# Moving two families of DMA issues off SyncE: in-projection spills to ScalarE, late modulation weights to GpSimd

## The chip, the cores and the metric

The kernel runs on one core of one Trainium2 chip. The metric is device time in microseconds (us); the shown figure is the median of three runs. Five instruction streams run beside each other and each is in order: PE (TensorE), DVE (VectorE), ACT (ScalarE), POOL (GpSimd) and SP (SyncE). A DMA is issued by one of the last three; the issue stands in that engine's stream like any other instruction and waits there for its semaphores.

## The reference

One block of a hybrid model, 512 tokens by 1024 channels, all in float32:

```
cond = silu(c)
mod = cond @ w_ada + b_ada                       # 6 x 1024: shift, scale, gate, twice
h = rms_norm(x, norm1) * (1 + scale1) + shift1
p = h @ w_in                                     # q,k,v | z | beta,a | RWKV columns | gate_a | gate_b
y_a = gated_deltanet(qkv, z, ...) @ w_branch_gdn # chunks of 64 tokens, 8 heads
y_b = rwkv7_time_mix(p_b, ...) @ w_branch_rwkv
x = x + gate1 * ((sigmoid(gl_a) * y_a + sigmoid(gl_b) * y_b) @ w_out)
h = rms_norm(x, norm2) * (1 + scale2) + shift2
x = x + gate2 * conv_glu(h, w_ffn_in, conv, w_ffn_out)
return rms_norm(x, norm_f)
```

## The kernel before

Everything is held transposed, channels on the 128 partitions and the 512 tokens along the free axis. A product of a weight tile with the activations is made of 24 matmuls of 128x128 by 128x512 (8 tiles of the inner dimension, 3 matmuls each): weights and activations are split into a high and a low part in fp32r, `whi`/`wlo` and `hh`/`hl`, and `mm3` (lines 182 to 191) issues high x high (L186), high x low (L189) and low x high (L190). A weight tile comes by a 512 KB DMA into `raw` (two buffers, L156); ACT makes `whi` (L145) and DVE makes `wlo` (L148).

The products form a queue, and `stream` works it off a few matmuls at a time: the chunk recurrences call `fill(n)` between their own small matmuls. So the recurrences of GatedDeltaNet (lines 742 to 788, steps L754, L762, L775, L776) and of RWKV-7 (lines 862 to 899, steps L868, L874, L887, L888) run inside the stream of products. Each recurrence is preceded by a triangular solve (`solve`, lines 544 to 610): its 32x32 blocks go out to DRAM and back in another layout (`lsc`, L556 and L559), DVE works 30 elimination steps (L567, L569), and the result makes a second trip through DRAM (`tsc`, `usc`).

Two things of this program are touched by the change:

- **The spills.** Four groups of products are not used at once: z (`zsc`), the two merge gates (`asc`, `bsc`) and the GatedDeltaNet branch (`ysc`), 28 tiles in all. `spill` copies the PSUM bank to a buffer `tmp_sp` on ACT (L404) and stores that to DRAM (L405); the loads back are L840 (`zsc`) and L944 to L946.
- **The late modulation weights.** Of the 48 modulation columns groups, 16 are made in the prologue. The other 32 come in halves through one single buffer `wada`: 64 times `ada_half` loads 256 KB (L208), and DVE multiplies by `cond` and sums (L209, an instruction of 128x512 and a short one that reads the sum). With one buffer, a load can't be issued before the L209 ahead of it is done.

The author's code gives an order, but the framework's scheduler sets the place of each instruction in its engine's stream, by its own model of their cost. An instruction whose issuer changes can so move on every engine. Between L817 and L842, named below, lies this work: L812 multiplies for the RWKV chunk matrices, DVE masks them (L817, L816), POOL clears parts of them (L578, L821), and DVE and ACT normalize the GatedDeltaNet output (L833), gate it with z (L842) and split it (L148 into `tmp_acc` and `tmp_sq`); this is the input of the branch products. A2 (L998) is a small vector of modulation factors.

Of the kernel before, what the change touches and what calls it, by code (L numbers as in the profile page):

```python
# [55 lines left out]
def body(ctx, tc, io, out, tap=lambda name, ap: None):  # L56
    nc = tc.nc
    pe, act, dve, pool, sp = nc.tensor, nc.scalar, nc.vector, nc.gpsimd, nc.sync
# [42 lines left out]
    def tmp(tag, bufs=2):  # L101
        return tp.tile([128, 512], F32, name=f"tmp_{tag}", tag=tag, bufs=bufs)
# [14 lines left out]
    def col(name, j=0, w=1):  # L117
        o = COLS[name][0] + j
        return cols[:, o:o + w]
# [85 lines left out]
    def ada_half(j, u):  # L205
        w = wp.tile([128, T], F32, name="wada", tag="wada")
        part = slice(T * u, T * u + T)
        sp.dma_start(w, io["w_ada"][j][:, part])  # L208
        i = dve.tensor_tensor_reduce(out=w, in0=w, in1=cond[:, part], scale=1.0,  # L209
                                 scalar=half[:, j:j + 1] if u else col("b_ada", j), op0=ALU.mult, op1=ALU.add,  # L210
                                 accum_out=(mod if u else half)[:, j:j + 1])
        if last["gate"] is not None:
            tc.add_manual_dep(i.ins, last["gate"].ins.name, after, reason="place")
            last["gate"] = None
# [15 lines left out]
    def stream():  # L230
        while queue:
            it = queue.pop(0)
            for _ in range(min(it["late"], len(ada_rest))):
                ada_half(*ada_rest.pop(0))
            for i, q in enumerate(it["pieces"]):
                for a in (it["pieces"][i:] + [b for nx in queue[:2] for b in nx["pieces"]])[:2]:
                    if a["w"] is None:
                        a["w"] = weights(a["src"], a["n"] * 128, a["spare"])
                if it["halves"]:
                    continue  # L240
                if i == 0:
                    p = it["psum"]()
                for k in range(q["n"]):
                    at = q["k0"] + k
                    mm3(p, q["w"], k, it["xs"][at], at == 0, at == it["n"] - 1)
                    if at == it["n"] - 1:
                        it["evac"](p)
                        done.add(it["label"])
                    yield
            for u in range(2 if it["halves"] else 0):  # L250
                part = slice(H * u, H * u + H)
                p = it["psum"]()[:, 0:H]
                for q in it["pieces"]:
                    for k in range(q["n"]):
                        at = q["k0"] + k
                        mm3(p, q["w"], k, [x[:, part] for x in it["xs"][at]], at == 0, at == it["n"] - 1)
                        yield
                it["evac"](p, u, part)
                done.add(it["label"])
# [141 lines left out]
    def spill(dst):  # L401
        def f(p):
            o = tmp("sp")
            act.copy(o, p)  # L404
            sp.dma_start(dst, o)  # L405
        return f

    kqs = slot2(0)
# [123 lines left out]
    def hs(e):  # L532
        return slice(64 * e, 64 * e + 64)
# [210 lines left out]
    for c in range(NC):  # L744
# [12 lines left out]
        for ct, e, r in heads():  # L757
            o = hs(1 - e)
# [7 lines left out]
        if c < NC - 1:  # L766
            p = q4(pc()[:, 0:256])
            for ct, e, r in heads():
                o = hs(1 - e)
# [226 lines left out]
    while ada_rest:  # L996
        ada_half(*ada_rest.pop(0))
# [167 lines left out]
```

## Time and profile before

| | |
|---|---|
| time, median of 3 runs | 939.75 us (938.65 to 940.68) |
| the profiled execution, its own time | 938.37 us |
| its span on the core | 936.4 us |
| PE busy | 878.2 us, 94% |
| DVE / ACT / POOL busy | 532.2 / 424.3 / 107.3 us |
| granted TensorE clock, mean | 0.98 |
| DMA queue 1 (all issues of SP) | 125.88 MB, 42.4% of 16 engines |

PE carries the program. The span is read as PE's work plus the places where PE stands; the first 17 us (loads and the first norm) and the last 8 us have a mostly idle PE, and the rest of its idle time lies in short gaps of about one us in the recurrences, the solves and the merge.

### The profile page before, as it was taken

The numbers are of one execution on the slowest core, as the hardware profiler recorded it, in microseconds if no ns is written. First come the engines' busy times: TensorE is split into PE (matmuls) and PEld (weight loads), VectorE is DVE, ScalarE is ACT, GpSimd is POOL, SyncE is SP. The second block draws the span as 40 slices with busy tenths as digits, with TensorE's granted clock in tenths as the row PEclk, the third lists the DMA queues.
The fourth block names the chain that finished last, engine by engine and source line by source line (L and its number), as shares of the span: only waits on it lengthen the run. The fifth ranks groups of instructions, "written<-read, shape, count | busy, mean of one in ns | idle before, by whom it ended". The sixth has DMA issues, their size and how long they took to land.

```text
span 936.4 us, 13900 instructions
## 1 busy us (share of the span) xinstructions
PE 878.2 (94%) x5459; PEld 687.0 (73%) x5459; DVE 532.2 (57%) x850; ACT 424.3 (45%) x691; POOL 107.3 (11%) x99
## 2 busy tenths in 40 slices
PE   2999989999999988999998999999999999999996
PEld 1886577676666666777665788888888888888885
DVE  5987859724796777245378537465444445332233
ACT  5368443734654838622466435343333333232231
POOL 1000310000361300001233320000000000010112
PEclk9999999998999989899999999999999999999998
DMA  9841254454233366744537542322332332533322
GB/s 340 284 161 57 79 138 158 130 138 137 89 91 100 86 219 225 185 143 159 176 120 255 178 153 83 106 97 90 100 103 90 96 108 90 176 100 101 101 85 90
DMA packets 81695, 126.77 MB, mean 135 GB/s; under 512 B 26109, under 2 KB 42877, under 8 KB 81566
## 3 DMA queue, kind: packets, MB, share of 16 engines
q1 hardware_dynamic: 81630, 125.88, 42.4%
q8 instruction: 43, 0.70, 0.3%
q14 instruction: 22, 0.18, 0.1%
HBM read 110.66 MB, written 14.68 MB: 134 GB/s over the span
## 4 chain that ended last, share of the span: by engine, by line
PE 70%; DVE 10%; ACT 8%; issue 6%; DMA 3%; POOL 2%; SPq 0%; DVEq 0%; ACTq 0%; POOLq 0%
PE ps_mm L186 19%; PE ps_mm L189 18%; PE ps_mm L190 18%; PE ps_pc L181 3%; DVE wlo L148 2%; ACT slot L615 2%; ACT tmp_rs L94 1%; PE ps_pc L186 1%; PE ps_pc L189 1%; PE ps_pc L190 1%; PE ps_pa L186 1%; ACT whi L145 1%; PE ps_pa L189 1%; PE ps_pa L190 1%; PE ps_pa L600 1%
## 5 line engine op out<-in xcount | busy, mean ns | idle before, releaser
L186 PE MATMUL ps_mm<-hh,whi 128*128 128x512 f32 (+1 forms) x714 | 291.2, 409 | 7.6 <-ACT hh L304 3.4
L190 PE MATMUL ps_mm<-hh,wlo 128*128 128x512 f32 (+1 forms) x714 | 280.8, 395 | 2.2 <-DVE wlo L148 2.2
L189 PE MATMUL ps_mm<-hl,whi 128*128 128x512 f32 (+1 forms) x714 | 280.8, 394 | 0.0
L148 DVE TENSOR_TENSOR wlo<-raw,whi 128x1024 fp32r<-128x1024 f32 (+2 forms) x140 | 161.1, 1151 | 184.5 <-ACT whi L145 178.2
L145 ACT CAST whi<-raw 128x1024 fp32r<-128x1024 f32 (+2 forms) x140 | 137.1, 979 | 246.5 <-PE ps_mm L189 188.0
L186 PEld LDWEIGHTS ps_mm<-hh,whi 128*128 128x128 f32 x714 | 135.4, 190 | 47.0 <-issue 7.0
L190 PEld LDWEIGHTS ps_mm<-hh,wlo 128*128 128x128 f32 x714 | 135.5, 190 | 34.2 <-DVE wlo L148 4.0
L189 PEld LDWEIGHTS ps_mm<-hl,whi 128*128 128x128 f32 x714 | 135.8, 190 | 29.9 <-issue 4.8
L186 PE MATMUL ps_mm<-slot,whi 128*128 128x512 f32 (+1 forms) x154 | 59.1, 385 | 2.7 <-ACT hh L145 1.5
L190 PE MATMUL ps_mm<-slot,wlo 128*128 128x512 f32 (+1 forms) x154 | 59.5, 386 | 1.8 <-DVE wlo L148 1.8
L189 PE MATMUL ps_mm<-slot,whi 128*128 128x512 f32 (+1 forms) x122 | 45.5, 373 | 0.2 <-DVE slot L148 0.2
L209 DVE CUSTOM_DVE_ANT_0 wada<-wada,cond,cols 128x512 f32<-128x512 f32 x32 | 25.0, 782 | 33.5 <-DMA wada<-in_w_ada 33.5
L190 PEld LDWEIGHTS ps_mm<-slot,wlo 128*128 128x128 f32 x154 | 29.7, 193 | 9.3 <-DVE wlo L148 4.2
L186 PEld LDWEIGHTS ps_mm<-slot,whi 128*128 128x128 f32 x154 | 29.7, 193 | 9.3 <-ACT hh L145 1.9
L186 PE MATMUL ps_mm<-slotd,whi 128*128 128x512 f32 (+1 forms) x96 | 36.4, 380 | 0.0
L190 PE MATMUL ps_mm<-slotd,wlo 128*128 128x512 f32 (+1 forms) x96 | 36.1, 376 | 0.0
L189 PE MATMUL ps_mm<-slotd,whi 128*128 128x512 f32 (+1 forms) x96 | 36.1, 376 | 0.0
L1040 DVE TENSOR_TENSOR tmp_sg<-tmp_acc,ps_mm 128x512 f32<-128x512 f32 x20 | 13.8, 688 | 35.6 <-PE ps_mm L190 35.5
L394 DVE SCALAR_TENSOR_TENSOR tmp_acc<-ps_mm,cols,tmp_acc 128x511 f32<-128x511 f32 (+2 forms) x44 | 32.8, 746 | 0.7
L973 POOL COPY tmp_rs<-tmp_sq 128x512 f32<-128x512 f32 x2 | 2.1, 1068 | 267.4 <-ACT tmp_sq L970 267.4
L94 ACT ACTIVATE tmp_acc<-tmp_acc 128x512 f32<-128x512 f32 x22 | 13.9, 631 | 41.5 <-DVE tmp_acc L394 41.4
L975 POOL TENSOR_TENSOR tmp_rs<-tmp_rs,tmp_sq 128x512 f32<-128x512 f32 x12 | 19.5, 1623 | 103.8 <-ACT tmp_sq L970 103.8
(266 smaller groups left out, 1286.7 us busy)
## 6 DMA issues: line engine op xcount, KB each, us to landing
raw<-in_w_in SPq DMA_DIRECT2D x40, 512.0 KB, 4.0
raw<-in_w_fi SPq DMA_DIRECT2D x37, 512.0 KB, 3.5
wada<-in_w_ada SPq DMA_DIRECT2D x64, 256.0 KB, 2.9
raw<-in_w_fo SPq DMA_DIRECT2D x16, 512.0 KB, 3.5
slot<-in_w_ada SPq DMA_DIRECT2D x10, 512.0 KB, 8.5
slot<-in_xT SPq DMA_DIRECT2D x16, 256.0 KB, 4.2
raw<-in_w_out SPq DMA_DIRECT2D x8, 512.0 KB, 3.6
raw<-in_w_in SPq DMA_DIRECT2D x8, 448.0 KB, 4.5
```

The costliest lines, as they stand in the source:

```text
L94: i = act.activation(*a, **k)
L145: i = act.copy(hi, src)
L148: j = eng.tensor_tensor(lo, src, hi.bitcast(F32), op=ALU.subtract)
L181: last["step"] = pe.matmul(*a, **k)
L186: i = pe.matmul(p, hi, xh, start=start, stop=False)
L189: pe.matmul(p, hi, xl, start=False, stop=False)
L190: pe.matmul(p, lo, xh, start=False, stop=stop)
L209: i = dve.tensor_tensor_reduce(out=w, in0=w, in1=cond[:, part], scale=1.0, scalar=half[:, j:j + 1] if u else col("b_ada", j), op0=ALU.mult ...
L394: dve.scalar_tensor_tensor(acc[:, i:], p[:, :T - i], w[:, taps - 1 - i:taps - i], acc[:, i:], op0=ALU.mult, op1=ALU.add)
L615: (act.copy if e == c or quiet else dve.tensor_copy)(place(e, 2 * b + c), p[hs(c), :, e, :])
L975: pool.tensor_tensor(sums[0], sums[0], sq, op=ALU.add)
L1040: dve.tensor_tensor(t, accs[j], p, op=ALU.mult)
```

## The change

The issuing engine of two DMA calls is another one. Sizes, buffers and computations are the same.

```
     def ada_half(j, u):
         w = wp.tile([128, T], F32, name="wada", tag="wada")
         part = slice(T * u, T * u + T)
-        sp.dma_start(w, io["w_ada"][j][:, part])
+        pool.dma_start(w, io["w_ada"][j][:, part])
...
     def spill(dst):
         def f(p):
             o = tmp("sp")
             act.copy(o, p)
-            sp.dma_start(dst, o)
+            act.dma_start(dst, o)
         return f
```

All 64 loads of `wada` stand in POOL's stream now, and all 28 spills in ACT's. The first load of `wada` needs nothing and stands near the start of POOL's stream. The scheduler moves DVE's L209 to earlier places as well: 19 of them stood behind the first L874 of the RWKV recurrence, and now none does.

On DVE, at the end of the GatedDeltaNet recurrence, the normalization (L833) and gating (L842) stood like this before; the `tmp_acc` and `tmp_sq` rows are the split that the branch products read:

```order
L209 ISA wada,mod<-wada,cond,half 128x512
L209 ISA mod 128x1
L833 SCALAR_TENSOR_TENSOR slotd_459<-slotd_459,cols,tmp_rs 128x512
L148 TENSOR_TENSOR wlo<-raw,whi 128x1024
L833 SCALAR_TENSOR_TENSOR slotd_459<-slotd_459,cols,tmp_rs 128x512 x3
L842 TENSOR_TENSOR tmp_rs<-slotd_459,tmp_sg 128x512 x2
L148 TENSOR_TENSOR tmp_acc<-tmp_rs,slot_2750 128x512 x2
L148 TENSOR_TENSOR wlo<-raw,whi 128x512
L842 TENSOR_TENSOR tmp_rs<-slotd_459,tmp_sg 128x512 x2
L560 TENSOR_SCALAR slot_2673<-slot_2673 128x1024
L148 TENSOR_TENSOR tmp_sq<-tmp_rs,slot_2750 128x512 x2
```

The same rows on DVE now, as far as the first two L842:

```order
L209 ISA wada,mod<-wada,cond,half 128x512
L209 ISA mod 128x1
L833 SCALAR_TENSOR_TENSOR slotd_459<-slotd_459,cols,tmp_rs 128x512 x2
L148 TENSOR_TENSOR wlo<-raw,whi 128x1024
L209 ISA wada,half<-wada,cond,cols 128x512
L209 ISA half 128x1
L833 SCALAR_TENSOR_TENSOR slotd_459<-slotd_459,cols,tmp_rs 128x512
L148 TENSOR_TENSOR wlo<-raw,whi 128x512
L833 SCALAR_TENSOR_TENSOR slotd_459<-slotd_459,cols,tmp_rs 128x512
L209 ISA wada,mod<-wada,cond,half 128x512
L209 ISA mod 128x1
L842 TENSOR_TENSOR tmp_rs<-slotd_459,tmp_sg 128x512 x2
```

Two L209 that were not there stand between the normalizations and the gating, and two more follow before the `tmp_sq` split. From the last L754 to that split there are 11 L209 where there were 6.

On POOL, at the same place in the program, the masks stood without a DMA between them before:

```order
L726 TENSOR_TENSOR slot_1357<-tmp_sg,slot_1357 128x512
L850 TENSOR_TENSOR slot_1792<-slot_1792,slot_1356 128x512
L578 MEMSET slotd_2469 32x32x32 x2
L821 AFFINE_SELECT slotd_1358<-slotd_1358 64x2048
L821 AFFINE_SELECT slot_2470<-slot_2470 64x2048
L561 AFFINE_SELECT slot_2673<-slot_2673 128x1024
```

POOL's rows now:

```order
L726 TENSOR_TENSOR slot_1357<-tmp_sg,slot_1357 128x512
L208 DMA wada<-in_w_ada 128x512 x2
L850 TENSOR_TENSOR slot_1792<-slot_1792,slot_1356 128x512
L208 DMA wada<-in_w_ada 128x512 x6
L578 MEMSET slotd_2469 32x32x32 x2
L821 AFFINE_SELECT slotd_1358<-slotd_1358 64x2048
L821 AFFINE_SELECT slot_2470<-slot_2470 64x2048
L208 DMA wada<-in_w_ada 128x512 x4
L561 AFFINE_SELECT slot_2673<-slot_2673 128x1024
L208 DMA wada<-in_w_ada 128x512 x14
```

The load behind the two L821 is the one that the second L209 of the DVE rows above (the one ahead of the third L833) reads.

On DVE, ahead of the first step of the RWKV recurrence (L874), there were two splits of weights and no L209 between them and the step:

```order
L209 ISA wada,half<-wada,cond,cols 128x512
L209 ISA half 128x1
L148 TENSOR_TENSOR wlo<-raw,whi 128x1024 x2
L874 TENSOR_SCALAR slotd_459<-ps_pc 64x256
L148 TENSOR_TENSOR wlo<-raw,whi 128x1024
```

Now the last five L209 of the program stand there, four of them one behind the other:

```order
L148 TENSOR_TENSOR wlo<-raw,whi 128x1024
L209 ISA wada,half<-wada,cond,cols 128x512
L209 ISA half 128x1
L209 ISA wada,mod<-wada,cond,half 128x512
L209 ISA mod 128x1
L209 ISA wada,half<-wada,cond,cols 128x512
L209 ISA half 128x1
L209 ISA wada,mod<-wada,cond,half 128x512
L209 ISA mod 128x1
L874 TENSOR_SCALAR slotd_459<-ps_pc 64x256
L148 TENSOR_TENSOR wlo<-raw,whi 128x1024
```

On PE, one whole product (24 matmuls) that stood behind the first triangular solve's L590 now stands ahead of it, and six matmuls of the second branch product stand ahead of the first that read `tmp_sq`.

More of the change, by code (lines that the diff above doesn't have):

```diff
@@ L207, in ada_half @@
         part = slice(T * u, T * u + T)
-        sp.dma_start(w, io["w_ada"][j][:, part])
+        pool.dma_start(w, io["w_ada"][j][:, part])
         i = dve.tensor_tensor_reduce(out=w, in0=w, in1=cond[:, part], scale=1.0,
@@ L404, in f @@
             act.copy(o, p)
-            sp.dma_start(dst, o)
+            act.dma_start(dst, o)
         return f
```

## The prediction, on record before the run

> **What bounds the kernel now.** I read the page first, then the busy time in stretches of 20 us, then the waits of PE, DVE and SP, and last the order of time around the places where the change moves something.
>
> ```profile
> PE 878.2 (94%) x5459; PEld 687.0 (73%) x5459; DVE 532.2 (57%) x850; ACT 424.3 (45%) x691; POOL 107.3 (11%) x99
> 0.00:20.00 20.00, 3.04 (x4) 1.34 (x5) 9.81 (x16) 12.18 (x17) 2.75 (x13) 1.00 0.94 335
> ...
> 260.00:280.00 20.00, 17.78 (x174) 12.06 (x173) 19.75 (x29) 10.92 (x21) 12.63 (x11) 1.00 0.34 104
> ...
> 320.00:340.00 20.00, 16.13 (x62) 11.88 (x61) 14.03 (x30) 11.35 (x18) 1.59 (x1) 0.83 0.51 165
> 360.00:380.00 20.00, 16.63 (x83) 11.65 (x81) 10.48 (x30) 19.33 (x47) 0.00 (x0) 1.00 0.75 205
> 400.00:420.00 20.00, 20.00 (x231) 15.18 (x229) 10.18 (x20) 5.32 (x10) 1.92 (x2) 1.00 0.41 141
> 500.00:520.00 20.00, 15.47 (x60) 10.26 (x59) 16.79 (x21) 13.13 (x21) 8.46 (x6) 1.00 0.78 266
> ```
>
> The columns of a stretch are PE, weight load, DVE, ACT and POOL busy, granted clock, DMA share and GB/s. PE is the bound: 58 us of the span are not PE, and 17 of those lie in the first 20 us. So little can be won. From 400 us on PE is full and DVE is half free; at 260 to 340 PE has gaps and DVE is the engine that sets them. What counts is therefore where DVE's work lies, not how much there is.
>
> ```profile
> DVE wada L209 <- DMA wada<-in_w_ada: 40.9, 25, 3.5
> SPq L405 <- ACT tmp_sp L404: 58.0, 24, 8.9
> ACT whi L145 <- DMA raw<-in_w_bg: 4.8, 2, 2.8
> wada<-in_w_ada SPq DMA_DIRECT2D x64, 256.0 KB, 2.9
> ```
>
> DVE already waits 40.9 us for the single `wada` buffer. SP stands 58.0 us at spills whose copy isn't done, but almost nothing waits behind it: the worst weight load costs ACT 4.8 us.
>
> **Place A, 294 to 334 us, carries the sum.** In order of time on DVE, with the two POOL rows that price a POOL instruction and the masks:
>
> ```profile
> 294.18 0.75 DVE L209 CUSTOM_DVE_ANT_0 wada<-wada,cond,cols 128x512 f32<-128x512 f32 x1 [0.51 <-DMA wada<-in_w_ada]
> ...
> 299.92 0.42 DVE L817 TENSOR_TENSOR slotd<-ps_pc,cons 128x256 f32<-128x256 f32 x1
> ...
> 302.54 0.33 SPq L208 DMA_DIRECT2D wada<-in_w_ada  x1
> ...
> 305.33 0.75 DVE L209 CUSTOM_DVE_ANT_0 wada<-wada,cond,half 128x512 f32<-128x512 f32 x1 [0.40 <-DMA wada<-in_w_ada]
> ...
> 312.44 0.76 DVE L209 CUSTOM_DVE_ANT_0 wada<-wada,cond,half 128x512 f32<-128x512 f32 x1 [0.44 <-DMA wada<-in_w_ada]
> ...
> 331.68 2.34 DVE L148 TENSOR_TENSOR tmp_sq<-tmp_rs,slot 128x512 fp32r<-128x512 f32 x2
> 332.42 0.50 PE L189 MATMUL ps_mm<-tmp_sq,whi 128*128 128x512 f32 x1 [2.24 <-DVE tmp_sq L148]
> ```
>
> ```profile
> 239.93 0.19 POOL L716 COPY pend<-tmp_acc 128x8 f32<-128x8 f32 x1 [1.14 <-ACT tmp_acc L94]
> 279.20 1.61 POOL L718 TENSOR_TENSOR tmp_rs<-slot,tmp_rs 128x512 f32<-128x512 f32 x1
> 311.33 1.95 POOL L578 MEMSET slotd<- 32x1024 f32 x2 [19.06 <-ACT slotd L816]
> 313.35 2.54 POOL L821 TENSOR_SCALAR_AFFINE_SELECT slotd<-slotd 64x2048 f32<-64x2048 f32 x1
> 315.96 2.99 POOL L821 TENSOR_SCALAR_AFFINE_SELECT slot<-slot 64x2048 f32<-64x2048 f32 x1
> ```
>
> From 294.18 to 312.44 lie five turns of the buffer, 18.26 us, so one turn P is 3.65: 0.75 for L209, 0.33 for SP's issue and 2.57 for the rest. DVE waits in each, so it is the loads that set the pace here, and PE ends up waiting for the split (2.24). On POOL the issue costs g in place of 0.33, and no row shows it. Bounds: 0.19 (the shortest POOL instruction) and 1.61 (one over 128x512). It is a whole POOL instruction but does no arithmetic over 128x512; I take the middle, g = 0.9, so P = 0.75 + 0.9 + 2.57 = 4.22 (3.51 to 4.93).
>
> The new order has 11 L209 where 6 stood. The first starts at 293.7, as its load is early now. The load of the eighth stands behind L578 and both L821, which POOL can start only after the load of the seventh and the last L817: 293.7 + 5P + 0.75 (L209) + 1.25 (three rows L816 and L817, 0.42 each) + 7.6 (311.33 to 318.95, the masks) + g + 2.57 = 327.9. Three more turns follow, 12.7, then L209 and both splits, 3.3: `tmp_sq` is done at 343.8, where it was done at 334.0. PE has six matmuls more to do meanwhile (1.4). A costs **+8.4** (g = 0.19: +2.3; g = 1.61: +14.8). Queued behind the POOL issue that waits are the masks, and behind those the next load; who waits is DVE, and for it PE.
>
> The Trainium skill (DMA: Bandwidth & Descriptors, "Latency and other measured facts") puts the first byte at about 0.6 us for a DMA from SP or ACT and about 1 us for one that GpSimd's software makes. No run here shows it yet; by its 0.4 as the whole difference P is an estimated 4.05, and A an estimated 6.9.
>
> **Place B, the first L874.** Four L209 now stand between a weight split and L874.
>
> ```profile
> 381.87 1.23 DVE L148 TENSOR_TENSOR wlo<-raw,whi 128x1024 fp32r<-128x1024 f32 x1 [4.90 <-ACT whi L145]
> 393.03 0.43 DVE L874 TENSOR_SCALAR slotd<-ps_pc 64x256 f32<-64x256 f32 x1 [9.94 <-ACT slot L873]
> 395.68 0.27 PE L181 MATMUL ps_pc<-slot,slot 128*64 128x64 f32 x1
> ```
>
> 383.1 + 3P + 0.75 + 0.43 = 396.9, and PE wants it at 395.7: **+1.3** (0 to +3.4). After this, no L209 is left, but PE was full there anyway, so those 19 moved L209 win nothing.
>
> **Place C, the first L762.** Eight L209 now stand one after another from the split at 187.42 to the first step of the GatedDeltaNet recurrence; PE has a product more to do before it, 24 matmuls at 0.227 (two rows of L186 are three matmuls apart, 0.68 us), 5.44.
>
> ```profile
> 187.00 0.39 PE L186 MATMUL ps_mm<-hh,whi 128*128 128x512 f32 x1
> 187.42 1.23 DVE L148 TENSOR_TENSOR wlo<-raw,whi 128x1024 fp32r<-128x1024 f32 x1 [3.34 <-ACT whi L145]
> 187.68 0.39 PE L186 MATMUL ps_mm<-hh,whi 128*128 128x512 f32 x1
> ...
> 214.64 0.91 PE L181 MATMUL ps_pc<-ck,slot 64*64 64x64 f32 x12
> ```
>
> 188.65 + 7P + 0.75 + 0.42 = 219.4 against 214.64 + 5.44 = 220.1: **0** (0 to +4.3). The cover is that one product; a turn of over 4.3 uses it up.
>
> **Place D, the decay masks.** The load of the fifth L209 stands behind POOL's third pair of L519.
>
> ```profile
> 102.83 1.61 POOL L519 TENSOR_SCALAR_AFFINE_SELECT tmp_sg<-tmp_sg 64x512 f32<-64x512 f32 x2 [1.42 <-ACT tmp_sg L94]
> 107.23 0.69 DVE L521 TENSOR_TENSOR slotd<-tmp_sg,beta 128x512 f32<-128x512 f32 x1 [0.55 <-POOL tmp_sg L519]
> 107.95 2.29 DVE L626 TENSOR_TENSOR slotd<-slotd,slot 64x2048 f32<-64x2048 f32 x1
> 111.71 1.09 PE L631 MATMUL ps_pa<-slotd 64*64 64x128 f32 x16 [1.03 <-DVE slotd L635]
> ```
>
> 104.44 + g + 2.57 = 107.9, then L209 and L521 (0.75 + 0.69): L626 starts at 109.35, 1.4 late, less three matmuls that PE now does first (0.7): **+0.7** (0 to +1.4).
>
> **The small terms.** The first `wada` load goes out at the start beside the loads of x, which PE's first matmul waits for: 0.262 MB at 335 GB/s, **+0.8** (0 to +0.8). The spills cost ACT 28 x 0.33 = 9.2 us. ACT has room nearly everywhere; on the path are the one ahead of the weight cast that PE waits for at 137 us, and three where ACT is at 19.33 of 20:
>
> ```profile
> L405 SPq DMA_DIRECT2D asc<-tmp_sp x8: 320/327/1142, 313.8 to 413.3; - x8
> ...
> 137.10 0.50 PE L186 MATMUL ps_mm<-hh,whi 128*128 128x512 f32 x1 [1.66 <-ACT whi L145]
> ```
>
> Four times 0.33, **+1.3** (0 to +3). What SP wins: weight loads no longer stand behind spills and `wada`. I give it **-1.0**, a fifth of PE's 4.5 idle us at 500 to 520 (0 to -6, with all of that and the gap at 137).
>
> Sum: 8.4 + 1.3 + 0 + 0.7 + 0.8 + 1.3 - 1.0 = 11.5. The profiled execution took 938.37, 1.4 below the median 939.75; 938.4 + 11.5 = 949.9. I forecast **950**.
>
> **Rivals.** What a measurement can tell from no change here is about 0.2%, 1.9 us.
>
> *A cheap POOL issue.* g near 0.2: A +2.3, the first load and the spills +2.1, SP -1: 942. For it: L716 takes 0.19. Against it: 1.61 for L718.
>
> *Faster: the freed SP queue.* SP's loads for the second solve come when their data are ready; at present DVE stands 2.30 for one and PE 2.24 behind it:
>
> ```profile
> 330.73 1.04 DVE L560 TENSOR_SCALAR slot<-slot 128x1024 f32<-128x1024 f32 x1 [2.30 <-DMA slot<-lsc_r]
> ```
>
> With that gap gone and half of 4.5 at 500 to 520, 938.4 - 2.2 - 2.2 = 934. It decides only if A costs nothing: nine turns stand in A's formula, and it is zero at P = 3.28, which leaves -0.04 for POOL's issue.
>
> *No change.* All of it lies beside PE's 94%: 938 to 940. It needs the same cheap issue, and the queue's gain to meet the rest.
>
> *Much slower: DVE and POOL in each other's way.* L727 takes 1.76 beside POOL's L726 and 0.68 alone:
>
> ```profile
> 262.02 1.76 DVE L727 TENSOR_TENSOR slotd<-slotd,tmp_acc 128x512 f32<-128x512 f32 x1
> 272.36 0.68 DVE L727 TENSOR_TENSOR slotd<-slotd,tmp_acc 128x512 f32<-128x512 f32 x1
> ```
>
> If each issue is held up by that 1.1, g = 2 and P = 5.3: A +18.1, B +4.5, C +6.8, D +1.8, the rest +1.1: 971. The Trainium skill (SBUF — State Buffer, "SBUF: two separate sides") says that GpSimd can't write a DMA's descriptors while DVE runs an instruction that holds both ports; the two L727 rows show the engines in each other's way, but no row shows it for an issue.
>
> **How the numbers follow.** Forecast 0.48; cheap issue 0.18; faster 0.13; no change 0.09; much slower 0.12. Faster by over 0.2%: 0.13; within: 0.10; slower: 0.77. The range of 938 to 966 leaves out most of the faster case and half of the much slower one, 0.19; its upper end is the sum of the upper bounds, 14.8 + 3.4 + 4.3 + 1.4 + 0.8 + 3 = 27.7.
>
> **What would show it.** The `wada` turns between L817: 4.2 apart if right, 3.65 or less if wrong. DVE's wait for `wada` well above 40.9. PE's wait for `tmp_sq` some 10 us in place of 2.9. The masks L821 after 318, and the eighth L209 about 9 us behind them at most. If DVE's waits for `wada` stay near 41 and PE's gap at `tmp_sq` shrinks, the forecast is wrong, and it is the price of POOL's issue that failed.

## The result, and the profile after

The changed kernel takes 970.59 us (median of 4 runs, 969.69 to 972.52), the kernel before beside it 939.2 us: a ratio of 1.034 (1.032 to 1.036). It is 31 us slower. The forecast of 950 us lies below that, and so does its whole range, which ends at 966. The profiled execution took 971.18 us with a span of 969.5, 33.1 us above the span of before, and the account below is made against that.

First the busy times, then three stretches of 20 us in the columns shown before, then the rows on `wada` and the first L874 from the waits (us in total, times, longest) and the DMA issues, then POOL's issue by itself (shortest, median and longest, in ns).

```profile
PE 884.8 (91%) x5459; PEld 690.6 (71%) x5459; DVE 533.9 (55%) x850; ACT 424.8 (44%) x691; POOL 137.1 (14%) x163
340.00:360.00 20.00, 13.31 (x54) 9.68 (x53) 13.05 (x31) 9.40 (x16) 3.15 (x5) 0.91 0.49 166
400.00:420.00 20.00, 15.21 (x295) 12.84 (x293) 4.18 (x9) 9.81 (x18) 2.08 (x4) 0.66 0.71 190
420.00:440.00 20.00, 15.85 (x164) 12.19 (x164) 6.91 (x12) 3.41 (x7) 0.92 (x2) 0.83 0.27 93
DVE wada L209 <- DMA wada<-in_w_ada: 94.8, 47, 5.4
POOL wada L208 <- DVE half L209: 125.3, 26, 38.5
PE ps_pc L181 <- DVE slotd L874: 4.2, 1, 4.2
wada<-in_w_ada POOLq DMA_DIRECT2D x64, 256.0 KB, 3.1
L208 POOL DMA_DIRECT2D wada<-in_w_ada x64: 538/538/710, 1.4 to 419.5; - x64
```

DVE's work is nearly the same (533.9 against 532.2 us), but it waits 94.8 us for `wada`, 47 times, where it waited 40.9 us, 25 times. PE's time outside its matmuls grew from 58.2 to 84.7 us (span less busy), and the same 5459 matmuls were busy 6.6 us longer; the mean granted clock is 0.971 where it was 0.980, and it is 0.66 in the stretch from 400 us, in which PE stops several times.

Where PE fell behind shows in rows that stand in both traces, behind waits that both have. First the kernel before (three such rows stand in the prediction); the last row, on L1067, is from the chain that ended last:

```profile
205.01 0.21 PE L600 MATMUL ps_pa<-slotd,tmp_sg 32*32 32x32 f32 x1 [0.67 <-ACT tmp_sg L595]
249.88 1.12 PE L729 MATMUL ps_pa<-tmp_sq,ones_r 128*128 128x512 f32 x2 [0.58 <-DVE tmp_sq L725]
364.44 0.66 PE L612 MATMUL ps_pa<-cons,slot 128*128 128x128 f32 x4 [0.40 <-ACT slotd L615]
385.34 0.21 PE L600 MATMUL ps_pa<-slotd,tmp_sg 32*32 32x32 f32 x1 [0.67 <-ACT tmp_sg L595]
462.19 0.51 PE L175 MATMUL ps_pa<-tmp_sp,ones_r 128*128 128x512 f32 x1 [0.43 <-POOL tmp_sp L148]
930.87 2.06 DVE slot L1067 x3
```

The same after:

```profile
114.80 1.09 PE L631 MATMUL ps_pa<-slotd 64*64 64x128 f32 x16 [1.26 <-DVE slotd L635]
217.64 0.21 PE L600 MATMUL ps_pa<-slotd,tmp_sg 32*32 32x32 f32 x1 [0.67 <-ACT tmp_sg L595]
229.43 0.90 PE L181 MATMUL ps_pc<-ck,slot 64*64 64x64 f32 x12 [2.85 <-DVE ck L762]
260.69 1.12 PE L729 MATMUL ps_pa<-tmp_sq,ones_r 128*128 128x512 f32 x2 [0.57 <-DVE tmp_sq L725]
383.77 0.66 PE L612 MATMUL ps_pa<-cons,slot 128*128 128x128 f32 x4 [0.41 <-ACT slotd L615]
409.19 0.26 PE L600 MATMUL ps_pa<-slotd,tmp_sg 32*32 32x32 f32 x1 [0.67 <-ACT tmp_sg L595]
424.49 0.37 PE L181 MATMUL ps_pc<-slotd,slot 128*64 128x64 f32 x1 [4.15 <-DVE slotd L874]
493.12 0.51 PE L175 MATMUL ps_pa<-tmp_sp,ones_r 128*128 128x512 f32 x1 [0.43 <-POOL tmp_sp L148]
961.94 2.06 DVE slot L1067 x3
```

| up to | PE (last: DVE) is late by | added in the stretch | forecast |
|---|---|---|---|
| decay masks, L631 | 3.1, less 0.7 of three matmuls moved ahead: 2.4 | 2.4 (start and place D) | 0.8 + 0.7 |
| first solve, L600 | 12.6, less 5.4 of the product moved ahead: 7.2 | 4.8 | no term |
| GatedDeltaNet recurrence, L729 | 10.8 | 3.6 (place C) | 0 |
| second solve, L612 | 19.3 | 8.5 (place A) | 8.4 |
| RWKV recurrence done, L175 | 30.9 | 11.6 (place B) | 1.3 |
| last L1067 | 31.1 | 0.2 | 0 |
| end of the span (969.5 less 936.4) | 33.1 | 2.0 | not in the sum |

Place B is where the forecast broke: 11.6 us where 1.3 was expected. It looks like this on DVE, with one row of POOL (not every row is shown):

```profile
392.54 0.19 DVE L569 TENSOR_TENSOR slot<-slot,pr 128x30 f32<-128x30 f32 x1
396.38 0.75 DVE L209 CUSTOM_DVE_ANT_0 wada<-wada,cond,cols 128x512 f32<-128x512 f32 x1 [3.65 <-DMA wada<-in_w_ada]
397.06 1.22 DVE L148 TENSOR_TENSOR wlo<-raw,whi 128x1024 fp32r<-128x1024 f32 x1
402.75 0.75 DVE L209 CUSTOM_DVE_ANT_0 wada<-wada,cond,half 128x512 f32<-128x512 f32 x1 [4.48 <-DMA wada<-in_w_ada]
403.43 1.22 DVE L148 TENSOR_TENSOR wlo<-raw,whi 128x1024 fp32r<-128x1024 f32 x1
408.23 0.75 DVE L209 CUSTOM_DVE_ANT_0 wada<-wada,cond,cols 128x512 f32<-128x512 f32 x1 [3.58 <-DMA wada<-in_w_ada]
414.42 0.75 DVE L209 CUSTOM_DVE_ANT_0 wada<-wada,cond,half 128x512 f32<-128x512 f32 x1 [5.43 <-DMA wada<-in_w_ada]
415.10 0.08 DVE L209 DVE_READ_ACCUMULATOR2_ANT mod<- 128x1 f32 x1
415.48 0.54 POOL L208 DMA_DIRECT2D wada<-in_w_ada  x1 [5.65 <-DVE mod L209]
418.48 0.75 DVE L209 CUSTOM_DVE_ANT_0 wada<-wada,cond,cols 128x512 f32<-128x512 f32 x1 [3.30 <-DMA wada<-in_w_ada]
423.21 0.75 DVE L209 CUSTOM_DVE_ANT_0 wada<-wada,cond,half 128x512 f32<-128x512 f32 x1 [3.98 <-DMA wada<-in_w_ada]
424.01 0.43 DVE L874 TENSOR_SCALAR slotd<-ps_pc 64x256 f32<-64x256 f32 x1
```

From the end of the solve's elimination to L874 DVE works 6.8 of 31.3 us (six L209 and two splits); the rest, 24.4, is six waits for loads, each asked for only when the L209 ahead of it is done. An undisturbed turn takes 4.06 us (414.42 to 418.48); those from 396 to 414 take 5.5 to 6.4, beside SP's loads for the solve and the next weights.

### The profile page after: what moved, and what is told of

It reads as the page before. It is cut to its first block, busy times and chain, and to the rows that moved or that the text cites. A ratio compares the mean times of both kernels' runs of the same rounds, so it can differ in the third digit from the quotient of the medians.

```text
span 969.5 us, 13903 instructions
## 1 busy us (share of the span) xinstructions
PE 884.8 (91%) x5459; PEld 690.6 (71%) x5459; DVE 533.9 (55%) x850; ACT 424.8 (44%) x691; POOL 137.1 (14%) x163
## 3 DMA queue, kind: packets, MB, share of 16 engines
q1 hardware_dynamic: 68382, 101.76, 33.1%
## 4 chain that ended last, share of the span: by engine, by line
PE 59%; issue 19%; DVE 9%; DMA 6%; POOL 4%; ACT 3%; SPq 0%; DVEq 0%; POOLq 0%; ACTq 0%
PE ps_mm L186 16%; PE ps_mm L189 16%; PE ps_mm L190 16%; DMA wada<-in_w_ada 4%; PE ps_pc L181 2%; POOL wada L208 2%; DVE wlo L148 1%; PE ps_pc L186 1%; PE ps_pc L190 1%; PE ps_pc L189 1%; DVE wada L209 1%; PE ps_pa L186 1%; PE ps_pa L189 1%; PE ps_pa L190 1%; DMA slot<-in_xT 1%
## 5 line engine op out<-in xcount | busy, mean ns | idle before, releaser
L208 POOL DMA_DIRECT2D wada<-in_w_ada x64 | 35.1, 549 | 253.6 <-DVE half L209 125.3
L209 DVE CUSTOM_DVE_ANT_0 wada<-wada,cond,half 128x512 f32<-128x512 f32 x32 | 25.6, 801 | 52.2 <-DMA wada<-in_w_ada 52.1
L209 DVE CUSTOM_DVE_ANT_0 wada<-wada,cond,cols 128x512 f32<-128x512 f32 x32 | 24.0, 750 | 42.9 <-DMA wada<-in_w_ada 42.7
L186 PEld LDWEIGHTS ps_mm<-slot,whi 128*128 128x128 f32 x154 | 29.2, 190 | 10.1 <-ACT slot L145 3.0
L1040 DVE TENSOR_TENSOR tmp_sg<-tmp_acc,ps_mm 128x512 f32<-128x512 f32 x20 | 13.8, 688 | 35.6 <-PE ps_mm L190 35.5
```

The lines of the kernel that those rows point to most:

```text
L186: i = pe.matmul(p, hi, xh, start=start, stop=False)
L208: pool.dma_start(w, io["w_ada"][j][:, part])
L1040: dve.tensor_tensor(t, accs[j], p, op=ALU.mult)
```

## The experiments

Theory *order*: the L209 that now stand ahead of the recurrences cost the time. Theory *issue*: POOL's issue and its DMA cost it wherever L209 stands. Theory *spills*: the stores in ACT's stream. The first four kernels part them; all of these ran on one chip against the kernel before (938.87 us).

**1. The whole change in the order of before.** DVE, PE and ACT are held in an order read from the built kernel before; POOL's and SP's orders are left to the scheduler:

```diff
+    for row in ORDER:
+        ...
+        for a, b in zip(row, row[1:]):
+            tc.add_manual_dep(in_order[b], a, after, reason="order")
```

> All of the change (modulation loads on POOL, spills on ACT), but DVE, PE and ACT are held in the order that the kernel before has, so that only the issuers differ. Theory order (the time went because the L209 moved ahead in DVE's stream, where DVE stands at a load that has only just been asked for, with the elimination steps and the recurrences queued behind): 942 us, 939 to 946, since a turn of the buffer is some 0.4 us longer (4.06 against 3.65) at the places where DVE waited before, and few of those were on PE's path. Theory issue (POOL's issue and its DMA are what costs, wherever L209 stands): 960 or more.

954.23 us (950.42 to 956.02), ratio 1.017 (1.015 to 1.020). Between the two theories: half of the loss goes with the order, and half stays with nothing but other issuers. PE does the same work in the same order as before, so its rows can be set side by side: in the profiled execution, the fastest of the four, it is 2.4 us late at the first L600, 4.7 at the first L729, 9.1 at the second solve's L612 and 10.1 at the L175 of the table above. It falls behind a little nearly everywhere up to the second solve. Its waits (calls of the held engines pass through a helper at L1177, which their rows name):

```profile
DVE wada L1177 <- DMA wada<-in_w_ada: 62.7, 37, 4.5
```

**2. The issuers of before in the order of the changed kernel.** The same rows from the changed kernel, with `sp.dma_start` in both places.

> The issuers of before (all on SP), but DVE, PE and ACT are held in the order of the changed kernel. Theory order: 960 us, 955 to 966: the L209 stand ahead of both recurrences as in the changed kernel, and some 25 turns that lie on the path are each 0.4 us shorter than POOL's. Theory issue: 948 or less.

982.63 us (982.06 to 984.32), ratio 1.047 (1.045 to 1.049). Worse than the changed kernel itself, by 12 us, where 10 us less was expected. The waits, SP's rows near the first L874 and DVE's row behind them show why:

```profile
DVE wada L1177 <- DMA wada<-in_w_ada: 101.0, 34, 13.8
SPq L405 <- ACT tmp_sp L1177: 110.1, 25, 12.3
424.14 0.33 SPq L405 DMA_DIRECT2D asc<-tmp_sp  x1
424.56 0.38 SPq L208 DMA_DIRECT2D wada<-in_w_ada  x1
427.51 0.75 DVE L1177 CUSTOM_DVE_ANT_0 wada<-wada,cond,cols 128x512 f32<-128x512 f32 x1 [7.16 <-DMA wada<-in_w_ada]
```

The load stands in SP's stream behind a spill whose copy ACT hasn't made. SP stood 12.3 us at this spill; the L209 ahead of the load ended at 419.22, so the load itself was held up 5.3 us. In this order the loads are on the path, and SP's queue holds them up more than POOL's slower issue does: the longest wait is 13.8 us, where it is 5.4 in the changed kernel. So the two effects don't add:

| | order of before | order of the changed kernel |
|---|---|---|
| issued by SP | 938.9 | 982.6 |
| loads by POOL, spills by ACT | 954.2 | 970.6 |

**3. Only the loads on POOL.**

```diff
-            act.dma_start(dst, o)
+            sp.dma_start(dst, o)
```

> Only the modulation loads go to POOL; the spills stay on SP. The scheduler puts 26 L209 ahead of the first L762 and all 64 ahead of the first L874, as in the changed kernel (17 and 47 before). Theory order: 970 us, 964 to 975, as slow as the changed kernel. Theory spills (the stores in ACT's stream cost the time): 955 or less.

972.3 us (968.08 to 973.59), ratio 1.035 (1.032 to 1.038): the whole loss. DVE waits 94.1 us for `wada`.

**4. Only the spills on ACT.**

```diff
-        pool.dma_start(w, io["w_ada"][j][:, part])
+        sp.dma_start(w, io["w_ada"][j][:, part])
```

> Only the spills go to ACT; the modulation loads stay on SP. The scheduler puts 17 L209 ahead of the first L762 and 48 ahead of the first L874, nearly as before. Theory order: 940 us, 937 to 942. Theory spills: 948 or more, 28 issues of 0.33 us on ACT (9.2 us) mostly on the path.

937.76 us, ratio 0.999 (0.998 to 1.001). Together, the spills on ACT and an SP without them change nothing that can be told; the run doesn't part the two. Theory spills falls; and since run 3 moves the L209 and run 4 hardly does, it is the issue on POOL that makes the scheduler move them.

**5. Place B undone.** In runs 5 and 6 L209 is held behind a step, with no other order given (the lines that collect the instructions in `ada_ops` and `mark` are left out here):

```diff
+    for at, n in (('B', 47),):
+        for o in ada_ops[n:]:
+            tc.add_manual_dep(o.ins, mark[at].ins.name, after, reason="held back")
```

> The changed kernel, but the 48th L209 and those behind it can't stand ahead of the first L874 (47 stand there, as in the kernel before; 64 in the changed one). Theory order: about 960 us, 957 to 963: the 10 us by which PE fell back further between the second solve and the first L874 go, since from there on PE is full and DVE half free. Rival conserved wait: DVE waits for as many loads later, inside the RWKV recurrence, and the time stays at 967 or more.

955.06 us (953.87 to 957.91), ratio 1.017 (1.015 to 1.019). 15.5 us come back, 5 more than expected, and the rival is out: the 17 L209 that went behind the first L874 cost nothing there that shows (PE is 14.4 us late at L175 and 13.7 at the first L978). They are the 17 that stood there in the kernel before: 47 of the 64 stood ahead of that step, so the 19 given ahead of the prediction, and in it, is two too high.

**6. Places C, A and B undone.** With `(('C', 17), ('A', 38), ('B', 47))`.

> The changed kernel with L209 held back at three places, so that as many stand ahead of each as in the kernel before: 17 ahead of the first L762, 38 ahead of the last L842, 47 ahead of the first L874 (26, 49 and 64 in the changed kernel). Nothing else is pinned. Theory order: 953 us, 949 to 956, as with the whole order of before, since the places of L209 are all that matters of the order. Rival: other moves of the scheduler (PE's product ahead of L590, A2) matter, and it stays above 960.

957.02 us (954.36 to 958.58), ratio 1.018 (1.015 to 1.021). That is 1 us above the range of the theory and below the 960 of the rival. There is no gain over run 5: with B undone, the moves at C and A are worth nothing. In the profiled executions PE reaches the first L729 at 256.4 in place of 261.7, but L175 at 479.0 in place of 476.6. 954 to 957 is what POOL's issue leaves with L209 where before had it.

**7 and 8. Two half buffers.** 128 loads of 128 KB, on POOL and on SP:

```diff
-        w = wp.tile([128, T], F32, name="wada", tag="wada")
-        part = slice(T * u, T * u + T)
+        w = wp.tile([128, H], F32, name="wada", tag="wada", bufs=2)
+        part = slice(H * u, H * u + H)
```

> The changed kernel with 128 loads of 128 KB into two buffers of 128x256 in place of 64 of 256 KB into one of 128x512: the same memory, and a load can be under way while DVE works on the other buffer. The 128 L209 cost DVE some 10 us more in all. Theory wait (what costs is DVE standing at a load that is asked for only when the L209 ahead is done): the waits for wada fall well below 94.8 us and the time to about 955 us, 945 to 963. Rival issue (what costs is POOL's issue, of which there are now twice as many): 970 or more.

> The kernel before with the same 128 loads of 128 KB into two buffers, all on SP. Theory wait: 936 us, 932 to 940: most of DVE's 40.9 us at loads goes, of which little lay on PE's path. Rival queue: SP's stream is the limit, and 64 more issues of 0.33 us ahead of weight loads make it 944 or more.

On POOL 976.79 us, ratio 1.040 (1.038 to 1.043); on SP 941.52 us, ratio 1.003 (1.001 to 1.005). My theory missed both ranges; on SP its rival, 944 or more, did not come true either. The waits on POOL:

```profile
DVE wada L209 <- DMA wada<-in_w_ada: 80.9, 61, 5.0
```

Half the size lands in 2.5 us where the whole took 3.1, so each half buffer still turns in nearly 4 us, and two of them bring hardly more per us than one whole buffer: the median distance of two L209, where the second waits for its load, is 1.99 us for 256 columns, so 3.98 for 512, where it is 4.37 in the changed kernel. All 128 stand ahead of the first L874, and DVE has more to do. The 970 that the rival named was passed too. Run 9 shows that 64 issues on POOL need not cost much; what 128 cost by their number alone is not tested.

**9 and 10. Small loads in the order of before.** The order is held as in run 1; `wada` is one lasting tile of which a load brings a quarter, and its product is scaled so that the stale columns stay finite. Three quarters of the modulation weights are left out, so the modulation values are not the reference's; the work of DVE, PE and ACT is the same:

```diff
-        pool.dma_start(w, io["w_ada"][j][:, part])
+        n = 128 if (j, u) != (16, 0) else T; pool.dma_start(w[:, :n], io["w_ada"][j][:, part][:, :n])
```

> All of the change, with DVE, PE and ACT held in the order of before (as the first of these experiments, 954 us), but each modulation load past the first brings 128 of its 512 columns, 64 KB in place of 256; the multiplication runs over the whole buffer, so DVE's work is the same and the modulation values are not the reference's. Theory turn (what is left of the loss at an equal order is that a turn of the buffer takes 4.06 us in place of 3.65): the smaller loads land about 0.8 us sooner, a turn is about 3.3, and the time is 936 to 942. Rival POOL stream (POOL's own work stands behind issues that wait for L209, or ACT's behind its spills): 949 or more, since as many issues stand there and wait.

> The kernel before, in its own order, with the same smaller loads: the control for the run with small loads on POOL. Theory turn: 932 to 938, as a turn falls to about 3 us and little of DVE's 40.9 us at loads lay on PE's path. Rival: no change from before, 938 to 940, if no turn lay on the path at all; then the 0.4 us a turn can't be what POOL costs.

On POOL 942.89 us (941.75 to 947.63), ratio 1.005 (1.003 to 1.008); on SP 937.6 us, ratio 0.999 (0.998 to 1.001).

```profile
DVE wada L209 <- DMA wada<-in_w_ada: 33.4, 19, 3.6
wada<-in_w_ada POOLq DMA_DIRECT2D x63, 64.0 KB, 2.2
```

With as many issues standing and waiting on POOL, 11.3 of run 1's 15.4 us go when the loads land sooner. The time is 1 us above the range of theory turn, and far below its rival's 949. PE, whose order is again that of before, is 2.7 us late at the first L600 and 2.8 at its last matmul: what run 1 lost between the two solves is gone. Of the 5.3 us left against run 10, 2.0 are the end of the program (below); 3.3 stay unexplained. On SP the turn was not on the path: run 10 gains nothing that can be told. Its expectation held that POOL's longer turn could then not be the cost either. Both results fit only if a turn of some 3.6 us just finds cover and one of some 4.1 doesn't; that is argued from the two runs, not shown. The smaller loads also move less data beside all other DMA; run 10 shows that this alone wins nothing on SP, and on POOL it is not parted from the turn.

**11 and 12. L209 held back further.** `(('C', 10), ('B', 26))` on the changed kernel, and on run 4's.

> The changed kernel with L209 held back further: 10 ahead of the first L762 and 26 ahead of the first L874 and of all that lies between (17 and 47 in before, 26 and 64 in the changed kernel); the other 38 run beside the full PE. Theory turn: the 16 us that are left with before's places come from some 47 turns ahead of the first L874, 0.34 each, so with 26 turns 948 us, 944 to 952. Rival: the 16 us are not tied to the number of turns, and it stays at 954 to 960 or rises, since 38 turns crowd the recurrence and the merge.

> Modulation loads on SP, spills on ACT (937.8 us in an earlier run), with the same holding back: 10 and 26. Theory turn: 932 us, 928 to 936, since the gaps of PE behind DVE's waits for wada in the two solves and recurrences go. Rival: the merge behind 490 us has no room for them, 940 or more.

On POOL 974.29 us, ratio 1.039 (1.036 to 1.042); on SP 943.27 us, ratio 1.006 (1.003 to 1.009). Both rivals came true. The theory holds up to the RWKV recurrence and fails behind it. PE's rows on POOL, the first to be set against 462.19 of before, the second in the merge, the third in the second norm:

```profile
471.55 0.50 PE L175 MATMUL ps_pa<-tmp_sp,ones_r 128*128 128x512 f32 x1 [0.79 <-POOL tmp_sp L148]
539.38 0.80 PE L190 MATMUL ps_mm<-hh,wlo 128*128 128x512 f32 x1 [3.93 <-DVE wlo L148]
588.90 0.70 PE L978 MATMUL ps_pa<-tmp_rs,one 128*128 128x256 f32 x2 [2.39 <-POOL tmp_rs L975]
```

The third row in the kernel before:

```profile
559.67 0.70 PE L978 MATMUL ps_pa<-tmp_rs,one 128*128 128x256 f32 x2 [0.26 <-POOL tmp_rs L975]
```

Up to L175 PE is 9.4 us late where the changed kernel is 30.9 late; by L978 it is 29.2 late. The 38 L209 that are left then make weight splits wait at the merge (ahead of the second row, DVE stood 2.96 us at a load of `wada`). On SP the same L175 stands at 455.86, 6.3 ahead of before, and the end 3.6 behind it. In this arrangement what a turn costs is moved, not saved; other places for the 38 were not tried. No kernel here beats the one before clear of noise.

## Why the prediction was wrong

**The direction and the mechanism** were right: DVE waits for single-buffered loads that the new order puts ahead of what PE needs.

**The turn.** P was put at 4.22 with an issue of 0.9 us, on a turn of 3.65 in the kernel before. DVE did not wait in each of those five turns, as the prediction has it: the L209 at 301.76, below, waits for nothing. The 3.65 is a mean that was about right all the same. In the changed kernel a turn between the L817 is 4.12 (309.94 to 326.41, four turns of L209). The sum held, not its parts: POOL's issue takes 0.54. The rest is a later start and a later landing. In the rows of place B the readout ends at 415.18 and POOL issues at 415.48; over 59 such issues the gap is 0.29 at least, 0.30 in the median. On SP the median over 56 is 0.03. Two rows of before:

```profile
301.76 0.74 DVE L209 CUSTOM_DVE_ANT_0 wada<-wada,cond,cols 128x512 f32<-128x512 f32 x1
302.43 0.08 DVE L209 DVE_READ_ACCUMULATOR2_ANT half<- 128x1 f32 x1
```

With the issue at 302.54 and the next L209 at 305.33, shown before, a turn of before was 3.57 there: 0.78 to the issue, 2.79 from it. After, it is 1.06 and 3.00. Of the 0.49 us, 0.28 lie ahead of the issue and 0.21 behind its start, as much as the issue itself is longer (0.54 against 0.33).
The Trainium skill (DMA: Bandwidth & Descriptors, "Latency and other measured facts") puts the first byte at about 1 us for GpSimd's DMA and about 0.6 us for one from SP or ACT, an estimated 0.4 us more. From issue to use these rows show 0.21, so the measurement is below that estimate.

**Place A** came out in size: 8.5 us against 8.4. The masks did stand between the seventh load and the eighth. But PE did not lose it where the forecast had it. Its wait for `tmp_sq`, which was to be some 10 us, was 2.9, as in the kernel before; PE had fallen behind already, in ten waits of over 0.25 us each between the first L812 and this split, 10.6 us together where the kernel before has 3.2; the longest is 2.7. That they add up to the forecast is in part luck. Rows of POOL, then two of PE's waits:

```profile
327.47 0.54 POOL L208 DMA_DIRECT2D wada<-in_w_ada  x1 [3.43 <-DVE half L209]
328.05 1.95 POOL L578 MEMSET slotd<- 32x1024 f32 x2
332.27 2.45 POOL L821 TENSOR_SCALAR_AFFINE_SELECT slot<-slot 64x2048 f32<-64x2048 f32 x1
334.68 0.56 POOL L208 DMA_DIRECT2D wada<-in_w_ada  x1
PE ps_pa L812 <- ACT slotd L818: 3.1, 2, 2.7
PE ps_mm L189 <- DVE tmp_sq L148: 2.9, 1, 2.9
```

Run 6 qualifies it further: with place B undone, taking the moved L209 out here and at C leaves the total as it was. A stretch's delay is not its worth.

**Place B is the step that failed**, 11.6 us where +1.3 (0 to +3.4) stood. Its rows give the parts. The chain was reckoned from the weight split, as if that came no later than PE; but the split stands behind two more L209 with waits of 3.65 and 4.48 and ended at 404.65, 21.5 us after its place before, when PE was 19.3 late: 2.2. From there on it counted three turns for four L209, as though the first load landed during the split; DVE waited 3.58 for that one too. And it took undisturbed turns: the four L209 and the step to L874 took 19.36 (404.65 to 424.01) where 3P and 0.75 make 13.41, so 5.95 with the missed wait, and 2.4 without. With the 1.3 that makes 9.5, PE's 28.8 at 424.49; the last 2.1 come in the steps just behind, in the stretch with a granted clock of 0.83. Its remark that behind the first L874 the moved L209 win nothing was right, and is the point: they cost nothing there (run 5, which gives back 15.5 us, more than this stretch lost).

**Place C** was +3.6 where 0 (0 to +4.3) stood, and the stretch ahead of it 4.8 where nothing was itemized: from the decay masks to the first L600 there are 18 L209 where 12 stood, and DVE's waits for `wada` there are 27.2 us in place of 3.0. Places were picked where the order shows a block of L209; the single ones inserted between a solve's steps were not counted.

**What the sum left out.** The longer turn was priced at four places only. Run 1 has no moved L209 at all and still loses 15.4 us: 2.0 at the end of the program, which had no term either, and the rest a little in nearly every stretch up to the second solve.

**The small terms.** Spills +1.3 and the freed SP -1.0: about 0 together (run 4). The start is 1.4 later (PE's first matmul at 15.41 in place of 13.98), but in the kernels with all modulation loads on SP it lies anywhere from 13.95 to 15.19, so that is no measure of it.

**The rivals.** "Much slower" named 971 and needed each issue held up by 1.1 us through DVE. The time came out, the mechanism did not: the 64 issues take 0.54 to 0.71 us, and L209 and DVE's total are nearly unchanged. "Faster" had one wait right: DVE's wait for a load ahead of L560 fell from 2.30 to 0.40 us, but DVE came there 19.5 us later (350.19 in place of 330.73), so it won nothing.
The Trainium skill (SBUF — State Buffer, "SBUF: two separate sides") ties that stall to DVE instructions holding both ports; no issue here shows it.

## What to carry to other kernels

A single-buffered load is a turn: work, wake the issuer, issue, land. Count every such turn ahead of a deadline, one by one, with the wait ahead of the first. Here half of the loss came from the deadline that the scheduler put the turns in front of, and most of the other half, with a turn 0.4 to 0.5 us longer, went when the loads landed sooner. Changing the issuing engine of a DMA changed the schedule of its consumers here, so compare the order of all engines and, to tell issue from order, hold one and change the other. A forecast that names where an engine will wait should be read back there: a sum can come out while the wait stands elsewhere.

## What the runs showed of the hardware

- A DMA issue on POOL took 0.54 us where one on SP took 0.33, and it began 0.30 us after DVE's releasing instruction ended where SP's began 0.03 us after.
- With the 64 loads on POOL, the program ended 2.0 us later after its last work: from the start of the last L1067 in the chain to the end of the span are 5.53 us before, 5.58 with spills on ACT and 5.58 with small loads on SP, but 7.56 after, 7.56 with small loads on POOL and 7.51 in run 5, though the last POOL load was issued hundreds of us earlier. The records of the traces show the step: POOL's closing DRAIN ends 0.07 us after POOL's last work in the kernel before and 5.32 us after it in all seven kernels with 64 loads on POOL. With 128 loads (run 7) it ends 1.89 us after it, and the end is only 0.6 us later (6.09). Why the drain lasts so long, and less with more loads, no run shows.
- A quarter of the bytes landed in some 70% of the time: on POOL 3.1 us for 256 KB, 2.5 for 128 KB and 2.2 for 64 KB.
